# A graph attention layer on one core: fewer filler matmuls ahead of the second counts, and row steps of the sort cut in other places

## Chip, core and metric

The kernel runs on one core of a Trainium2 chip. The metric is the device time of one execution in microseconds (us), lower is better. TensorE is PE in the rows, its weight loads PEld; VectorE is DVE, ScalarE is ACT, GpSimd is POOL, SyncE is SP. A letter q behind an engine's name means its sequencer.

## What is computed

The layer has 4096 nodes with 64 features, 50,000 edges and 4 heads. Each edge carries its source's projected row to its target with the weight exp(leaky(s + d)), and the sums are divided by the sums of the weights:

```python
x_proj[h] = x @ weight[h]
src_att = np.sum(x_proj[h, src_nodes] * att_src[h], axis=-1)
dst_att = np.sum(x_proj[h, dst_nodes] * att_dst[h], axis=-1)
edge_scores[h] = src_att + dst_att
edge_scores = np.where(edge_scores > 0, edge_scores, 0.2 * edge_scores)
output[h, dst] += np.exp(edge_scores[h, i]) * x_proj[h, src]
total = np.sum(np.exp(edge_scores[h, edges_to_dst]))
output[h, dst] /= (total + 1e-8)
```

## The kernel before

Edges become one number each (a key) and are put in order twice, so that all that follows are dense matmuls. The order of instructions on each engine is the order of the source: the part is written under a manual schedule, and the semaphores between engines are set from what each instruction reads and writes.

**First sort.** 128 partitions hold up to 512 keys each. `rows` (L342) sorts each partition's keys on VectorE: fours, then merges with `merge(k)` (L242), k from 3 to 7 and at last 9, where merge k joins sorted pieces into pieces of 2^k columns. A merge step is a MIN and a MAX between two sets of columns. It is issued as three instructions: MIN over the right part of the pieces, MAX over all, MIN over the left part (`left` pieces lie in the left part). So each instruction has another one between itself and the one whose output it needs first. `runs` (L368) then merges the rows of 4 partitions: ScalarE scales two parts of the columns by a sign (L376), VectorE shuffles (L380), combines (L383), and goes through steps j = 8 to 0 (`cross`, L364, three instructions a step by `apart`, L213; or `half`, L205, a MIN and a MAX of 256 columns each), with transpositions (`turn`, L358, in two parts of 384 and 128 columns). The keys go to DRAM.

**Second sort** (`group`, L529). Four indirect DMAs fetch `raw` (L522). `wide` (L305) sorts halves of 256 columns on VectorE, its last two steps over both halves (L319), and calls `merge(9)`; `runs` merges 8 partitions. Beside it ScalarE counts keys below 32 bounds, one pass (L422) for each, into the columns of `sgn`. TensorE has nothing to do between the score matmuls (L609) and these counts. When pass 25 is done (`WARM`), `busy` (L1065) issues one small matmul that waits for it (L1069) and then `EARLY` filler matmuls of 512 columns (L1071), whose result nobody reads; then the counts matmul (`counts`, L428, L432), which needs all 32 passes, and `LATER` more fillers.

**From the counts to the blocks.** The last steps of `runs` in the second sort (L399 to L405) are `half` steps, and behind each stands one small VectorE instruction of another kind: first `st.count` (L463), which reads the counts out of PSUM, then the fields of the first block's keys (L1079, L1082, L1083), then the start of the windows (L468, L470, L471). ScalarE casts the fields to `tb` (L1084), TensorE spreads them over all partitions (L684, 12 of 16 tiles first), ScalarE copies them to `bc` (L686), VectorE compares them to one-hot matrices `oh` (L699, L701). The sorted keys go out as `ki`, and POOL fetches `win` (L522) with indirect DMAs behind their store. VectorE takes win apart (L628 to L633), the result is stored to `gat_bins` and loaded back broadcast as `bc` for the blocks 2 and on (L673).

**Blocks.** 32 blocks of 128 target nodes follow in a pipeline: one-hot matrices on VectorE, gathering matmuls (L718 to L720), exp and casts on ScalarE (L730, L732), products (L752), sums on TensorE (L816), division and store. From block 2 on each takes the same time.

Of the kernel before, what the change touches and what calls it, by code (L numbers as in the profile page):

```python
# [16 lines left out]
OP = mybir.AluOpType  # L17
# [13 lines left out]
FINE = 2  # L31
PARTS = (slice(L // 4, L), slice(0, L // 4))
WARM = 25
EARLY = 28
REST = 2
LATER = 17
KPAD = float(1 << 24)
LOW = 80
HIGH = 24
# [5 lines left out]
def av(a, off, *dims):  # L45

    return dataclasses.replace(a, offset=a.offset + off, ap=[list(a.ap[0])] + [list(d) for d in dims])
# [3 lines left out]
def kernel(ctx: ExitStack, tc: tile.TileContext, x: bass.AP, edge_index: bass.AP,  # L51
                         weight: bass.AP, att_src: bass.AP, att_dst: bass.AP, out: bass.AP):
    nc = tc.nc
    V, S, G, T = nc.vector, nc.scalar, nc.gpsimd, nc.tensor
# [46 lines left out]
    def bits(name, shift, mask):  # L101
        i = cst.tile([P, 1], I32, name=f"{name}_i")
        f = cst.tile([P, 1], F32, name=f"{name}_f")
        V.tensor_scalar(out=i[:], in0=pidx[:], scalar1=shift, scalar2=mask, op0=OP.logical_shift_right,
                        op1=OP.bitwise_and)
        G.tensor_copy(out=f[:], in_=i[:])
        return f
# [6 lines left out]
    for j in range(3):  # L114
        f = bits(f"b{j}", j, 1)
# [73 lines left out]
    class Sorter:  # L189
# [52 lines left out]
        def merge(self, k, at=0, ns=1, left=0, top=L, way=None, steps=(1, 9), meanwhile=()):  # L242


            n = 1 << k
            q, third = n // 4, n // 8
            one, two, three = way or ((self.cur + i) % 4 + 1 for i in range(3))
            segs = ((left, ns), (0, left)) if left else ((0, 1),)

            def compare(s, d, op, lower, upper, *dims, out=None):  # L250
                if out is None:
                    out = av(d, upper if op == OP.max else lower, *dims)
                V.tensor_tensor(out=out, in0=av(s, lower, *dims), in1=av(s, upper, *dims), op=op)  # L253

            for i in range(max(steps[0], 1), min(steps[1], k) + 1):
                h = n >> i
                if i == 1:
                    s, d, apart = self.a[self.cur], self.a[one], (one - two) * L
                    if k == 3:
                        for lower, op in ((q, OP.min), (q, OP.max), (0, OP.max), (0, OP.min)):  # L260
                            o = lower + (op == OP.max) * h
                            compare(s, d, op, lower, lower + h, [n, ns], [1, q],
                                    out=av(self.a[one if q <= o < 3 * q else two], o, [n, ns], [1, q]))
                    elif left:
                        low = lambda f, e: compare(s, d, OP.min, at + n * f, at + n * f + h, [n, e - f], [q, 2], [1, q],
                                                   out=av(self.a[two], at + n * f, [n, e - f], [apart + q, 2], [1, q]))
                        low(*segs[0])
                        compare(s, d, OP.max, at, at + h, [n, ns], [q, 2], [1, q],
                                out=av(d, at + h, [n, ns], [q - apart, 2], [1, q]))
                        low(*segs[1])  # L270
                    else:
                        compare(s, d, OP.min, at + q, at + 3 * q, [1, q])
                        if top < at + n:
                            compare(s, d, OP.max, at, at + h, [1, q])
                            compare(s, self.a[two], OP.max, at + q, at + 3 * q, [1, top - at - 3 * q])
                        else:
                            compare(s, d, OP.max, at, at + h, [q, 2], [1, q], out=av(d, at + h, [q - apart, 2], [1, q]))
                        compare(s, self.a[two], OP.min, at, at + h, [1, q])
                    if k > 2:
                        ends = 1 if top < at + n else 2  # L280
                        e = (at, [n, ns], [n - third, ends], [1, third])
                        S.copy(out=av(self.a[three], *e), in_=av(self.a[two], *e))
                    for f in meanwhile:
                        f()
                    self.cur = one
                    continue
                s, self.cur = self.a[self.cur], three if i % 2 else two
                d = self.a[self.cur]
                m = min((1 << (i - 1)) - 1, -(-(top - at - h) // (2 * h)))
                pairs = lambda op, f, e, a, b: compare(s, d, op, at + n * f + h * (2 * a + 1), at + n * f + h * (2 * a + 2),  # L290
                                                       [n, e - f], [2 * h, b - a], [1, h])
                if left:
                    pairs(OP.min, *segs[0], 0, m)
                    pairs(OP.max, 0, ns, 0, m)
                    pairs(OP.min, *segs[1], 0, m)
                elif i == 2:
                    pairs(OP.min, 0, 1, 0, m)
                    pairs(OP.max, 0, 1, 0, m)
                else:
                    c = 1 << (i - 3)  # L300
                    pairs(OP.min, 0, 1, 0, c)
                    pairs(OP.max, 0, 1, 0, m)
                    pairs(OP.min, 0, 1, c, m)

        def wide(self, alone, load, between, meanwhile):  # L305

            k = 8
            way = 1, 2, 3
            for at in (0, L // 2):
                self.cur = 0  # L310
                load(at)
                self.merge(k, at, way=way, steps=(1, alone))
            between()
            for i in range(alone + 1, k + 1):
                s, self.cur = self.a[self.cur], way[2] if i % 2 else way[1]
                d, h, n = self.a[self.cur], 1 << (k - i), 1 << k
                for o, op, f, e in ((0, OP.min, 0, 1), (h, OP.max, 0, 2), (0, OP.min, 1, 2)):
                    dims = [n, e - f], [2 * h, n // (2 * h) - 1], [1, h]
                    V.tensor_tensor(out=av(d, n * f + h + o, *dims), in0=av(s, n * f + h, *dims),  # L319
                                    in1=av(s, n * f + 2 * h, *dims), op=op)  # L320
            self.merge(9, meanwhile=meanwhile)

        def fours(self, n, then):
# [18 lines left out]
        def rows(self, n, then, meanwhile):  # L342

            w8, w128 = -(-n // 8) * 8, n // 128 * 128
            assert 0 < n - w128 <= 8 and w128 == 3 * 128
            ways = {3: (2, 4, 1), 4: (2, 3, 4), 5: (2, 1, 4), 6: (3, 2, 1), 7: (3, 4, 1)}
            self.fours(w8 // 4, then)
            for k in range(3, 8):
                w = w8 if k <= 3 else w128
                self.merge(k, 0, w >> k, 2 if k == 7 else 192 >> k, meanwhile=meanwhile[k],  # L350
                           way=ways[k])
                assert k not in (3, 7) or self.cur == 1
            self.apart(7, mirror=True, right=True)
            for j in range(6, -1, -1):
                self.apart(j, w128 if j > 2 else w8, 128, right=True)
            self.merge(9, top=w8, meanwhile=meanwhile[9])
# [11 lines left out]
        def runs(self, size, then, skey, to=None, fine=0, between=()):  # L368
# [4 lines left out]
            s, z = self.step()  # L373
# [4 lines left out]
            for c in PARTS:  # L378
                c = slice(L - c.stop, L - c.start)
                V.stream_shuffle(out=z[:, c], in_=s[:, c], mask=[p ^ 1 for p in range(32)])  # L380
            d = self.step()[1]
# [3 lines left out]
            s, d = self.step()  # L385
# [10 lines left out]
            todo = list(between)  # L396
            for j in range(8, fine, -1):
                if todo:
                    self.half(j)  # L399
                    todo.pop(0)(self.a[self.cur])  # L400
                else:
                    self.cross(j)
            s, d = self.step()
            d, h = to or d, 1 << fine
            for c in (L // 2, 0):  # L405
                for o, op in ((0, OP.min), (h, OP.max)):
                    V.tensor_tensor(out=av(d[:], c + o, [2 * h, L // (4 * h)], [1, h]),
                                    in0=av(s[:], c, [2 * h, L // (4 * h)], [1, h]),
                                    in1=av(s[:], c + h, [2 * h, L // (4 * h)], [1, h]), op=op)
# [119 lines left out]
    def group(pool, pp, start, between=(), busy=None, scores=None):  # L529
# [18 lines left out]
        def then():  # L548
# [4 lines left out]
            if between:  # L553
                busy(EARLY, (sel2[:], sgn[:, WARM:WARM + 1]))
            st.ps = counts(pp, sgn, 8 * NI, [sel2[:]])
            if between:
                busy(LATER)

# [89 lines left out]
    class Blocks:  # L648
# [20 lines left out]
        def load(self, b, parts=((0, NT),)):  # L669
            if b < ND:  # L670
                t = self.bcp.tile([P, 2 * NT * W2], BF16, name="bc")
                for t0, n in parts:
                    nc.sync.dma_start(out=t[:, t0 * PW:(t0 + n) * PW],  # L673
                                      in_=dataclasses.replace(bin_dram[b], offset=bin_dram[b].offset + t0 * PW,
                                                              ap=[[0, P], [1, n * PW]]))
                self.bc[b] = t
# [523 lines left out]
```

## Time and profile before

| | us |
|---|---|
| median of 3 runs | 259.88 (258.58 to 260.5) |
| the profiled execution's own time | 257.67 |
| its span, first to last instruction | 255.9 |
| granted TensorE clock, mean over the span | 0.891 of full speed |
| busy: PE 200.9, DVE 238.9, ACT 201.8, POOL 44.7 | |

Some 1.8 us of the profiled execution lie outside the span. Times in the rows are counted from the span's start. The work up to about 104 us is sorting, and the blocks fill the rest.

### The profile page before, as it was taken

To read this page: it belongs to the slowest core of one execution; us is meant where nothing else is said; L and a number is where in the kernel's file an instruction comes from. 1 tells how busy PE (TensorE), PEld (TensorE's weight loads), DVE (VectorE), ACT (ScalarE), POOL (GpSimd) and SP (SyncE) were. 2 spreads that over 40 slices of the span, in tenths; PEclk is the share of its full clock that TensorE was granted. 3 is DMA by queue.
4 is the path that set the end of the run, shared out by engine and by line. 5 is a ranking of instruction groups with operands and counts; after the bars stand their busy time and mean duration, and the time that the engine had idled before them with its cause. 6 is when DMAs were issued, how large, how long until landed. Compare 5 with 4: busy or idle time off the path is not lost.

```text
span 255.9 us, 6908 instructions
## 1 busy us (share of the span) xinstructions
PE 200.9 (79%) x2539; PEld 178.4 (70%) x2539; DVE 238.9 (93%) x682; ACT 201.8 (79%) x523; POOL 44.7 (17%) x97
## 2 busy tenths in 40 slices
PE   0004669999200599878999999999999999999995
PEld 0003339999200245667999999999999999999994
DVE  7999999928999978989999999999999999999993
ACT  2774579005889935997999999999999999999981
POOL 7788000042000000584000007500000000000000
PEclk9999985555555589999999999999999999999999
DMA  4005000010000001189768677687767768675012
GB/s 125 0 2 186 0 3 3 0 62 21 1 0 0 0 0 45 41 305 409 269 256 300 247 270 289 233 318 246 286 251 241 303 226 327 250 298 220 23 44 68
DMA packets 12422, 39.43 MB, mean 154 GB/s; under 512 B 2208, under 2 KB 7904, under 8 KB 8800
## 3 DMA queue, kind: packets, MB, share of 16 engines
q1 hardware_dynamic: 10752, 36.84, 39.4%
q10 hardware_dynamic: 928, 1.51, 1.7%
q0 software_dynamic: 704, 0.59, 1.0%
q8 instruction: 21, 0.34, 0.5%
q14 instruction: 17, 0.14, 0.2%
HBM read 33.96 MB, written 4.98 MB: 152 GB/s over the span
## 4 chain that ended last, share of the span: by engine, by line
PE 57%; DVE 27%; ACT 7%; DMA 5%; issue 2%; POOL 0%; DVEq 0%; SPq 0%; POOLq 0%; ACTq 0%
PE acc L816 20%; DVE sorted L253 11%; PE ps L719 10%; DVE sorted L240 7%; PE ps L720 6%; PE ps L718 6%; PE pt L911 5%; ACT junk L422 5%; PE warm L1071 5%; PE pt L896 3%; DMA bc<-gat_bins 2%; DVE oh L699 1%; DVE val L752 1%; DMA eS<-in_edge_index_dram 1%; ACT bc L686 1%
## 5 line engine op out<-in xcount | busy, mean ns | idle before, releaser
L732 ACT CAST xs<-ps 128x1176 bf16<-128x1176 f32 (+1 forms) x96 | 103.2, 1076 | 0.0
L752 DVE TENSOR_TENSOR val<-xs,val 128x3072 bf16<-128x3072 bf16 (+2 forms) x64 | 75.1, 1173 | 0.7
L816 PE MATMUL acc<-val,xs 128*128 128x264 bf16 x496 | 66.4, 276 | 0.7 <-DVE val L752 0.7
L718 PE MATMUL ps<-xa,oh 128*128 128x68 bf16 x512 | 51.7, 194 | 2.5 <-ACT xs L732 0.9
L816 PEld LDWEIGHTS <-xs 128*128 128x128 bf16 x496 | 46.2, 98 | 6.7 <-DVE val L752 0.8
L719 PE MATMUL ps<-adb,oh 128*128 128x132 bf16 x512 | 49.6, 220 | 0.0
L718 PEld LDWEIGHTS <-oh 128*128 128x128 bf16 x512 | 43.7, 97 | 2.9 <-DVE oh L699 1.8
L719 PEld LDWEIGHTS <-oh 128*128 128x128 bf16 x512 | 40.8, 97 | 3.0 <-issue 2.3
L699 DVE TENSOR_SCALAR oh<-bc,pF 128x3328 bf16<-128x3328 bf16 (+4 forms) x38 | 36.1, 951 | 1.9 <-ACT bc L686 1.0
L720 PE MATMUL ps<-xa,oh 128*128 128x68 bf16 x512 | 36.3, 194 | 0.4 <-DVE oh L701 0.4
L730 ACT ACTIVATE ex<-ps 128x48 bf16<-128x48 f32 (+1 forms) x192 | 33.0, 243 | 4.2 <-PE ps L719 1.5
L240 DVE TENSOR_TENSOR sorted<-sorted 128x192 f32<-128x192 f32 (+2 forms) x141 | 34.4, 326 | 0.0
L253 DVE TENSOR_TENSOR sorted<-sorted 128x128 f32<-128x128 f32 (+22 forms) x157 | 30.1, 270 | 0.4 <-ACT junk L422 0.4
L720 PEld LDWEIGHTS <-oh 128*128 128x128 bf16 x512 | 28.6, 97 | 0.9 <-DVE oh L701 0.5
L609 PEld LDWEIGHTS scores<-uv,xT 64*128 64x128 f32 x128 | 27.6, 318 | 0.4 <-issue 0.4
L609 PE MATMUL scores<-uv,xT 64*128 64x4 f32 x128 | 27.7, 353 | 0.0
L422 ACT ACTIVATE junk<-kr,nb 128x512 f32<-128x512 f32 x32 | 23.1, 722 | 0.9
L701 DVE TENSOR_SCALAR oh<-bc,pF 128x1664 bf16<-128x1664 bf16 (+4 forms) x38 | 22.4, 591 | 0.0
L432 PE MATMUL cnt_ps<-sgn,sel 128*128 128x17 f32 (+1 forms) x10 | 2.2, 346 | 22.1 <-DVE sorted L253 22.1
L911 PE MATMUL pt<-Wbd,aT 128*128 128x128 f32 x124 | 19.0, 275 | 0.0
L432 PEld LDWEIGHTS cnt_ps<-sgn,sel 128*128 128x128 f32 x10 | 2.2, 300 | 22.2 <-issue 22.0
L1069 PE MATMUL warm<-sgn,sel 128*128 128x1 f32 x2 | 0.6, 364 | 20.4 <-ACT junk L422 20.4
(161 smaller groups left out, 280.8 us busy)
## 6 DMA issues: line engine op xcount, KB each, us to landing
bc<-gat_bins SPq DMA_DIRECT2D x28, 1024.0 KB, 5.6
out_dram<-res SPq DMA_DIRECT2D x32, 128.0 KB, 2.3
xf<-in_x_dram ACTq DMA_DIRECT2D x1, 1024.0 KB, 5.8
bc<-gat_bins SPq DMA_DIRECT2D x1, 768.0 KB, 4.6
bc<-gat_bins SPq DMA_DIRECT2D x1, 640.0 KB, 5.1
bc<-gat_bins SPq DMA_DIRECT2D x1, 384.0 KB, 3.9
gat_sorted<-sorted SPq DMA_DIRECT2D x2, 128.0 KB, 1.7
gat_sorted<-ki SPq DMA_DIRECT2D x2, 128.0 KB, 1.8
```

What stands on the lines that cost most here:

```text
L240: V.tensor_tensor(out=out, in0=in0, in1=in1, op=op)
L253: V.tensor_tensor(out=out, in0=av(s, lower, *dims), in1=av(s, upper, *dims), op=op)
L422: todo = [lambda b=b: S.activation(out=junk[:], in_=v, func=ACTF.Sign, bias=nbnd[:, b:b + 1], scale=1.0, accum_out=sgn[:, b:b + 1]) for b ...
L609: T.matmul(out=scores[:, k * NB + b, :], lhsT=nodes(b), rhs=uv[:, k, :], start=(k == 0 and b == 0), stop=True, skip_group_check=True)
L699: V.tensor_scalar(out=av(oh[:], *e), in0=av(bc[:], *e), scalar1=pF[:, 0:1], scalar2=None, op0=OP.is_equal)
L718: kinds = [lambda i, t, **how: T.matmul(out=ps[:, i, P:P + XC], lhsT=hot(2 * t + 1), rhs=xa[:, t, :], **how), lambda i, t, **how: T.matmul ...
L719: lambda i, t, **how: T.matmul(out=ps[:, i, 0:S0], lhsT=hot(2 * t), rhs=adb[:, b, :], **how),
L720: lambda i, t, **how: T.matmul(out=ps[:, i, P:P + XC], lhsT=hot(2 * NT + t), rhs=xa[:, NR + t, :], **how)]
L730: S.activation(out=av(ex[:], 2 * (k * H * NT + t0), [2, n], [2 * NT, H], [1, 2]), in_=av(ps[:], P, [PW, n], [1, H], [0, 2]), func=ACTF.Exp ...
L732: S.copy(out=xs[:, t0:t0 + n, 0:P + XC], in_=ps[:, 0:n, 0:P + XC])
L752: V.tensor_tensor(out=av(val, t0 * AW, [VW, H * n], [1, Din]), in0=av(xs, S0 + t0 * XW, [XW, n], [0, H], [1, Din]), in1=av(val, t0 * AW + ...
L816: T.matmul(out=acc[:, 0:AW], lhsT=xs[:, t, 0:P], rhs=val[:, t, :], start=(t == 0), stop=(t == NT - 1), **how)
```

## The change

Two constants and four places that cut instructions differ:

```diff
-EARLY = 28
+EARLY = 14
-LATER = 17
+LATER = 18
@@ merge(): the last step of a merge of 9
                     pairs(OP.min, 0, 1, 0, c)
                     pairs(OP.max, 0, 1, 0, m)
+                    if k == 9 and i == k:
+                        pairs(OP.min, 0, 1, c, 3 * c)
+                        c *= 3
                     pairs(OP.min, 0, 1, c, m)
@@ wide(): its last step
-                for o, op, f, e in ((0, OP.min, 0, 1), (h, OP.max, 0, 2), (0, OP.min, 1, 2)):
...
+                m = n // (2 * h) - 1
+                ends = ((m // 2 + 1, m), (0, m // 2 + 1)) if i == k else ((0, m),)
+                for o, op, f, e, a, b in ((0, OP.min, 0, 1, 0, m), (h, OP.max, 0, 2, 0, m),
+                                          *((0, OP.min, 1, 2, a, b) for a, b in ends)):
...
@@ rows(): the pieces in the left part
-                self.merge(k, 0, w >> k, 2 if k == 7 else 192 >> k, meanwhile=meanwhile[k],
+                self.merge(k, 0, w >> k, (192 if k < 5 else 256) >> k, meanwhile=meanwhile[k],
@@ runs(): the first of the steps that have other work behind them
-                    self.half(j)
+                    self.cross(j) if j == 8 else self.half(j)
```

- There are 14 fillers instead of 28 between the small matmul that waits for pass 25 and the counts, and 18 instead of 17 behind the counts.
- In the merges of 5 and 6 the left part has 8 of 12 and 4 of 6 pieces instead of half of them. The merge of 7 has 2 of 3 in both kernels.
- The last MIN of the last step is cut in two in both merges of 9 and at the end of `wide`.
- The first step behind the last transposition of the second sort is `cross(8)`: MIN of columns 128 to 255 against 384 to 511, MAX of all, MIN of the rest.

The instructions of ScalarE, GpSimd and SyncE and all DMAs stand as before. What follows of the changed kernel is five lines further down in the source (L468 there is L463 here).

VectorE behind the last transposition of the second sort, before the change (`sorted` are the sort's buffers, `cnt_ps` the counts in PSUM; a bracket names the engine whose semaphore is waited for):

```order
L362 STREAM_TRANSPOSE sorted<-sorted 128x384 [waits DVE_49]
L362 STREAM_TRANSPOSE sorted<-sorted 128x128 [waits DVE_49]
L209 TENSOR_TENSOR sorted<-sorted 128x256 [waits DVE_49]
L209 TENSOR_TENSOR sorted<-sorted 128x256
L463 TENSOR_SCALAR cnt<-cnt_ps 128x33 [waits PE_49]
L209 TENSOR_TENSOR sorted<-sorted 128x2x128 [waits DVE_49]
```

The same place after the change:

```order
L367 STREAM_TRANSPOSE sorted<-sorted 128x384 [waits DVE_49]
L367 STREAM_TRANSPOSE sorted<-sorted 128x128 [waits DVE_49]
L240 TENSOR_TENSOR sorted<-sorted 128x128 [waits DVE_49]
L240 TENSOR_TENSOR sorted<-sorted 128x256 [waits DVE_49]
L240 TENSOR_TENSOR sorted<-sorted 128x128
L468 TENSOR_SCALAR cnt<-cnt_ps 128x33 [waits PE_49]
L209 TENSOR_TENSOR sorted<-sorted 128x2x128 [waits DVE_49]
```

Two instructions of 256 columns became three of 128, 256 and 128, and the first of them reads only what the first transposition wrote.

VectorE at the end of the second merge of 9, before the change:

```order
L253 TENSOR_TENSOR sorted<-sorted 128x64 [waits DVE_49]
L253 TENSOR_TENSOR sorted<-sorted 128x255 [waits DVE_49]
L253 TENSOR_TENSOR sorted<-sorted 128x191
L380 STREAM_SHUFFLE sorted<-sorted 128x384 [waits DVE_49]
L380 STREAM_SHUFFLE sorted<-sorted 128x128
L383 SCALAR_TENSOR_TENSOR sorted<-sorted,sig_104 128x384 [waits DVE_49,Activation_49]
```

The same place after the change:

```order
L253 TENSOR_TENSOR sorted<-sorted 128x64 [waits DVE_49]
L253 TENSOR_TENSOR sorted<-sorted 128x255 [waits DVE_49]
L253 TENSOR_TENSOR sorted<-sorted 128x128
L253 TENSOR_TENSOR sorted<-sorted 128x63
L385 STREAM_SHUFFLE sorted<-sorted 128x384 [waits DVE_49]
L385 STREAM_SHUFFLE sorted<-sorted 128x128 [waits DVE_49]
L388 SCALAR_TENSOR_TENSOR sorted<-sorted,sig_104 128x384 [waits DVE_49,Activation_49]
```

The MIN of 191 columns became two of 128 and 63, and the first shuffle reads nothing of the second; the SCALAR_TENSOR_TENSOR waits for ScalarE (Activation) as before.

## Rows read from the trace of the kernel before

**Rows 1.** Chain of waits, 85.9 to 113 us: start us, us, what

```profile
86.58 8.33 PE warm L1071 x28
...
99.49 2.79 ACT bc L686 x2
...
106.55 2.00 DMA gat_bins<-tb
...
108.57 3.91 DMA bc<-gat_bins
...
112.50 0.55 DVE oh L699
```

**Rows 2.** PE in order of time: start us, us, line, operation, count

```profile
86.44 4.80 PE L1071 MATMUL warm<-identb 128*128 128x512 bf16 x11
91.08 3.83 PE L1071 MATMUL warm<-identb 128*128 128x512 bf16 x17
94.75 0.30 PE L432 MATMUL cnt_ps<-sgn,sel 128*128 128x33 f32 x2
94.97 3.83 PE L1071 MATMUL warm<-identb 128*128 128x512 bf16 x17
98.63 1.47 PE L684 MATMUL ps<-tb,identb 128*128 128x256 bf16 x12
```

**Rows 3.** Stretches: length, PE, PEld, DVE, ACT, POOL busy, PEclk, DMA share, GB/s

```profile
91.00:92.00 1.00, 1.00 (x6) 0.45 (x5) 1.00 (x5) 0.84 (x3) 0.00 (x0) 0.97 0.00 0
112.00:114.00 2.00, 1.10 (x22) 0.94 (x20) 1.40 (x4) 2.00 (x8) 1.83 (x6) 1.00 1.03 433
```

**Rows 4.** ACT in order of time: last counting pass, cast of the fields

```profile
91.68 0.18 ACT L422 ACTIVATION_READ_ACCUMULATOR junk<-kr,nb 128x1 f32 x1
97.12 0.41 ACT L1084 CAST tb<-t 128x256 bf16<-128x256 int32 x1 [5.25 <-DVE t L1083]
```

**Rows 5.** DVE in order of time, 82 to 106 us, in brackets idle time and releaser

```profile
82.10 0.77 DVE L362 STREAM_TRANSPOSE sorted<-sorted 128x384 f32<-128x384 f32 x2
82.79 0.79 DVE L240 TENSOR_TENSOR sorted<-sorted 128x128 f32<-128x128 f32 x3
...
92.27 0.77 DVE L362 STREAM_TRANSPOSE sorted<-sorted 128x384 f32<-128x384 f32 x2
93.08 0.76 DVE L209 TENSOR_TENSOR sorted<-sorted 128x256 f32<-128x256 f32 x2
95.09 0.19 DVE L463 TENSOR_SCALAR cnt<-cnt_ps 128x33 f32<-128x33 f32 x1 [1.25 <-PE cnt_ps L432]
...
99.40 0.89 DVE L407 TENSOR_TENSOR ki<-sorted 128x128 int32<-128x128 f32 x4
...
102.30 0.62 DVE L699 TENSOR_SCALAR oh<-bc,pF 128x1536 bf16<-128x1536 bf16 x1 [0.39 <-ACT bc L686]
...
105.84 0.22 DVE L628 TENSOR_SCALAR t<-win 128x128 int32<-128x128 int32 x1
```

**Rows 6.** The first fetch of win on POOL, and the four fetches' landing times

```profile
102.88 0.95 POOL L522 DMA_INDIRECT win<-gat_sorted,to  x1 [43.72 <-DMA gat_sorted<-ki]
DMA to landing us min/median/max: 2.5/3.0/6.3
```

**Rows 7.** Ends of wide and of the second merge of 9: DVE and ACT in order of time

```profile
64.46 0.62 DVE L319 TENSOR_TENSOR sorted<-sorted 128x254 f32<-128x254 f32 x2
65.11 0.63 DVE L253 TENSOR_TENSOR sorted<-sorted 128x128 f32<-128x128 f32 x2
71.30 0.91 ACT L376 ACTIVATE sorted<-sorted,sig 128x384 f32<-128x384 f32 x2 [0.92 <-DVE sorted L253]
72.00 0.88 DVE L383 SCALAR_TENSOR_TENSOR sorted<-sorted,sig 128x384 f32<-128x384 f32 x2
```

**Rows 8.** Stretches of the merges of 6 and of 7, VectorE alone

```profile
15.55:18.86 3.31, 3.31 (x20) 1.00 0.02 0
18.86:22.76 3.90, 3.90 (x22) 1.00 0.75 264
```

More of the change, by code (lines that the diff above doesn't have):

```diff
@@ L316, in wide @@
                 d, h, n = self.a[self.cur], 1 << (k - i), 1 << k
-                for o, op, f, e in ((0, OP.min, 0, 1), (h, OP.max, 0, 2), (0, OP.min, 1, 2)):
-                    dims = [n, e - f], [2 * h, n // (2 * h) - 1], [1, h]
-                    V.tensor_tensor(out=av(d, n * f + h + o, *dims), in0=av(s, n * f + h, *dims),
-                                    in1=av(s, n * f + 2 * h, *dims), op=op)
+                m = n // (2 * h) - 1
+                ends = ((m // 2 + 1, m), (0, m // 2 + 1)) if i == k else ((0, m),)
+                for o, op, f, e, a, b in ((0, OP.min, 0, 1, 0, m), (h, OP.max, 0, 2, 0, m),
+                                          *((0, OP.min, 1, 2, a, b) for a, b in ends)):
+                    at, dims = n * f + h * (2 * a + 1), ([n, e - f], [2 * h, b - a], [1, h])
+                    V.tensor_tensor(out=av(d, at + o, *dims), in0=av(s, at, *dims), in1=av(s, at + h, *dims), op=op)
             self.merge(9, meanwhile=meanwhile)
```

## Prediction

> **What bounds the kernel now.** I read the chain of waits first. From 86 us it runs through the fillers: 28 of them for 8.33 us, and then, over the spread fields, ScalarE's `bc`, the store to gat_bins and the load back, to the one-hot of block 2 at 112.50 [rows 1]. From there on block follows block, so what shifts that one-hot shifts the end. In time order, PE begins its fillers at 86.44; ten steps to the start of the eleventh and one more bring it to 91.08, 0.42 us each; the 17 from there to the counts at 94.75 take 0.216 each [rows 2]. The granted clock rose between them: 0.97 over 91 to 92 us [rows 3]. So the fillers serve to raise the clock from 1.2 to 2.4 GHz, and 17 of the 28 ran after it had risen. What the counts need was long there: ScalarE's last pass ended at 91.68 + 0.18 = 91.86 [rows 4], 2.9 us before the counts began. VectorE, which reads them, was ready about 93.8 and idled 1.25 us until 95.09 [rows 5]. Behind the counts PE ran 17 fillers to 98.63 [rows 2], though the fields it spreads next were cast at 97.12 + 0.41 = 97.53 [rows 4]: a second wait, of 1.1 us.
>
> **Fillers, 28 to 14.** The first eleven run to 91.08, three more at 0.216 to 91.73. The counts then wait for ScalarE (91.86) and start at about 91.90, 2.85 earlier; with their 0.30 the result is there by 92.2. VectorE is then late next, not PE.
>
> **The step behind the last turn.** `half(8)` starts 93.08 - 92.27 = 0.81 after its transpositions start. A `cross` behind a turn already stands in this trace: it starts 82.79 - 82.10 = 0.69 after them, because its first MIN overlaps the second transposition (it starts 0.08 before that ends, `half` 0.04 after) [rows 5]. Its three instructions last 0.79; an instruction that waits for nothing starts about 0.09 before the end, so 0.70 to the next. With nothing else changed VectorE reads the counts at 92.27 + 0.69 + 0.70 = 93.66 instead of 95.09. An instruction more on 512 columns costs 0.03 to 0.10: two last 0.76, three 0.79, four 0.89 [rows 5], mean 0.065; in this step it is inside the 0.79.
>
> **The other cuts of the sort** move everything before that by a little.
> - End of `wide`: the merge started 65.11, 0.03 after the MIN ended at 65.08 [rows 7], so it lost about 0.12 against an overlap of 0.09. With a second half in between the loss goes and 0.065 comes: -0.05.
> - End of the merges of 9: the shuffles can start earlier, but the combine at 72.00 waits also for ScalarE's first part, which starts 71.30, when the last MIN is done [rows 7]. A cut MIN ends 0.065 later, so ScalarE and the combine do: +0.07 in each sort, +0.14 if nothing gives. The bounds are -0.06 each (if the combine were held by the shuffles alone) and +0.10.
> - Two to one in the merges of 5 and 6: the merge of 6 takes 3.31 for 6 steps, 0.552 a step, the merge of 7, which has this cut already, 3.90 for 7, 0.557 [rows 8]. Eleven steps at a difference of 0.005 are 0.06; I take nothing, bounds -0.1 and +0.1.
>
> Sum -0.05 + 0.14 = +0.09, bounds -0.3 and +0.3. The counts are read at 93.75: -1.34 us. They are ready at 92.2 or, ScalarE's passes shifting by the same 0.09, 92.3, so 1.4 us cover this.
>
> The Trainium skill, VectorE: DVE Perf Modes, section The DRAIN you can't avoid, speaks against these cuts: the flush behind each VectorE instruction comes with or without a semaphore, so one should count instructions and not waits. By it the cuts in `wide` and behind the turn would gain none of their 0.12, the counts would be read 0.24 later, and the sum below would be -1.5. Rows 5 and 7 disagree: the distance behind an instruction was 0.04 or -0.08 by whether the next needed its output.
>
> **From the counts to block 2.** Two branches shift differently.
> - Spread. The cast ends at 97.53 - 1.34 = 96.19. Fillers: the first follows the counts' start by 0.22, 92.2, and 18 at 0.215 (17 took 98.63 - 94.97 = 3.66) end at 96.07. The spread starts at about 96.23 instead of 98.63: -2.40. The eighteenth filler costs nothing since the cast is later still; without that cover it costs 0.22. ScalarE's copies and the second one-hot (102.30) follow, and VectorE would reach L628 at 105.84 - 2.40 = 103.44.
> - Windows. L628 needs `win`, fetched from the sorted keys behind `ki` (99.40). That is VectorE's branch and gains only 1.34. The fetch was issued at 102.88 and lands 2.5 later at the least [rows 6]: 105.38, so it had up to 0.46 to spare before L628 at 105.84. Now it lands at 104.04, and L628 waits for it until 104.08: -1.76. If it had landed just in time, L628 gains 1.34 only. I take 2.5, since this is the first of four fetches and the later ones find the queue used.
>
> The store (2.00) and the load (3.91) [rows 1] start on L628 and move with it; before the load's end VectorE idled, so nothing else is late there. Sum: 1.8 us less. Against the profiled execution that is 257.67 - 1.8 = 255.9. The median is 2.2 us above that execution; the stage is the same, so I take the 1.8 off the median: 258.1, 0.7% less. A measurement of this kernel can tell about 1%, or 2.6 us, from no change.
>
> **Rivals.**
> - *The window binds fully.* If `win` landed only at 105.84, or the keys' store and fetch take longer in their new place, the gain is 1.34 or less: 258.5 to 259. For it: no row gives this fetch's own landing. Against: the least of four is 2.5.
> - *The clock rises at another moment.* A rise 0.42 later turns a filler of 0.216 into one of 0.42, so it delays the counts of before by 0.21, while the changed kernel hides it until 14 fillers at 0.42 (86.44 + 5.91 = 92.35) and the counts are done at 92.7, still ahead of 93.75. A rise 1.6 later makes the gain 1.8 + 0.8 = 2.6, 257.3; 1.6 earlier makes it 1.0, 258.9. For it: the runs of before differ by 1.9 us. One trace shows only one moment.
> - *Too few fillers, slower.* If the clock rises only after more work than 14 fillers and the counts, or is taken back because of the gap before the counts, the 18 later fillers take 18 x 0.42 = 7.6 and the spread starts at 99.8 instead of 98.63, +1.2; the spread and the first gathers, 1.5 us of PE work [rows 2] and as much again, at half the clock add 1.5 to 3: 262.6 to 264. It decides from a rise later than about 95. Against: the clock rose while the eleventh filler ended, and it held through 112 to 114 us with PE busy only 1.10 of 2.00 [rows 3]; the gap before the counts is under 0.2 us.
> - *The cuts of the sort cost more than they gain* (0.3): 258.4, inside the range.
>
> The Trainium skill, TensorE: Matmul & The Clock Gate, Part 1, says that the point at which the clock is released varies between runs of one kernel, as the monitor does not start with the kernel. By it the second rival is real in both directions; no trace here shows a second moment.
>
> **How the numbers follow.** Forecast (gain of 1.4 to 2.4): 0.58. Window binds or other small gain (0.3 to 1.4): 0.16. Late rise, gain above 2.4: 0.17. No gain within 0.3, as with an early rise and a full window: 0.04. Too few fillers: 0.05. Faster by over 1% needs 2.6 us: the late rise and the noise of the two medians at the edge of the forecast, 0.22. Slower: 0.05. Same: 0.73. The range 256.8 to 259.4 takes in gains from 0.5 to 3.1.
>
> **What would show it.** In the changed profile: 14 fillers from about 86.5, the last ones at 0.216; counts within 0.2 us of ScalarE's last pass; VectorE without idle time before it reads them, about 93.7; the spread directly behind the cast at about 96.2; and VectorE idle about 0.6 before L628 (now five lines further down), waiting for `win`. The gain at the counts should be 1.3 and at the first one-hot of block 2 1.8. Wrong would be: fillers of 0.42 behind the counts, an idle VectorE before the counts, or a one-hot of block 2 that moved by under 1 us.

## The result, and the profile after

The changed kernel takes 255.66 us (255.41 to 258.57, 19 runs) where the kernel before, timed beside it, takes 259.19 (258.44 to 260.5, 19 runs): a ratio of 0.9867, 95% interval [0.9847, 0.9887], or 3.5 us less. The forecast was 1.8 us less, 258.1, with a range from 256.8 to 259.4. The two profiled executions, 257.67 before and 255.53 after, differ by 2.14 only. So there are two questions: did the stage move as worked out, and where does the rest of the 3.5 us come from?

The chain of waits after, over the stretch of [rows 1] (columns as there):

```profile
86.79 4.71 PE warm L1076 x14
...
92.56 3.89 PE warm L1076 x18
...
97.19 2.79 ACT bc L691 x2
...
101.65 2.43 DMA win<-gat_sorted,to
...
105.07 1.53 DMA gat_bins<-tb
...
106.62 3.72 DMA bc<-gat_bins
...
110.37 0.59 DVE oh L704
```

A fetch of `win` stands in the chain now, which it did not before, and the one-hot of block 2 comes at 110.37 instead of 112.50: 2.13 earlier, as much as the two executions differ by. TensorE (PE) in order of time answers to [rows 2]:

```profile
86.65 4.85 PE L1076 MATMUL warm<-identb 128*128 128x512 bf16 x14
92.18 0.38 PE L437 MATMUL cnt_ps<-sgn,sel 128*128 128x33 f32 x2 [0.68 <-issue]
92.39 4.05 PE L1076 MATMUL warm<-identb 128*128 128x512 bf16 x18
96.34 1.47 PE L689 MATMUL ps<-tb,identb 128*128 128x256 bf16 x12
```

The counts start 2.57 us earlier than in [rows 2] and the spread 2.29. The clock, by stretches as in [rows 3]:

```profile
89.00:90.00 1.00, 1.00 (x3) 0.30 (x2) 1.00 (x4) 0.97 (x3) 0.00 (x0) 0.50 0.00 0
90.00:91.00 1.00, 1.00 (x6) 0.51 (x5) 1.00 (x6) 0.97 (x3) 0.00 (x0) 0.98 0.00 0
```

It rose from 1.2 to 2.4 GHz about 90.0, some 1 us earlier than in [rows 3]. ScalarE's last pass and cast, as in [rows 4]:

```profile
91.89 0.19 ACT L427 ACTIVATION_READ_ACCUMULATOR junk<-kr,nb 128x1 f32 x1
...
95.89 0.41 ACT L1089 CAST tb<-t 128x256 bf16<-128x256 int32 x1 [3.81 <-DVE t L1088]
```

The cast ends at 96.30 and the spread follows at 96.34: the second wait of [rows 2] is gone too. VectorE (DVE), as in [rows 5] and [rows 7]:

```profile
65.27 6.21 DVE L253 TENSOR_TENSOR sorted<-sorted 128x128 f32<-128x128 f32 x27
...
72.16 0.88 DVE L388 SCALAR_TENSOR_TENSOR sorted<-sorted,sig 128x384 f32<-128x384 f32 x2
...
92.45 0.76 DVE L367 STREAM_TRANSPOSE sorted<-sorted 128x384 f32<-128x384 f32 x2
93.14 0.78 DVE L240 TENSOR_TENSOR sorted<-sorted 128x128 f32<-128x128 f32 x3
93.84 0.18 DVE L468 TENSOR_SCALAR cnt<-cnt_ps 128x33 f32<-128x33 f32 x1
...
104.17 0.36 DVE L633 TENSOR_SCALAR t<-win 128x128 int32<-128x128 int32 x1 [0.50 <-DMA win<-gat_sorted,to]
```

No idle time stands in front of the counts' read (1.25 us in [rows 5]), and 0.50 us in front of L633, waiting for `win`. Both were forecast.

### The profile page after: what moved, and what is told of

Same layout as the page of the kernel before. It is cut to its first block, busy times and chain, and to the rows that moved or that the text cites. A ratio compares the mean times of both kernels' runs of the same rounds, so it can differ in the third digit from the quotient of the medians.

```text
span 253.7 us, 6886 instructions
## 1 busy us (share of the span) xinstructions
PE 198.3 (78%) x2526; PEld 177.2 (70%) x2526; DVE 239.1 (94%) x686; ACT 201.6 (79%) x523; POOL 44.0 (17%) x97
## 4 chain that ended last, share of the span: by engine, by line
PE 56%; DVE 27%; ACT 7%; DMA 4%; issue 4%; DVEq 0%; SPq 0%; ACTq 0%
PE acc L821 21%; DVE sorted L253 12%; PE ps L724 11%; DVE sorted L240 7%; PE ps L725 6%; PE ps L723 6%; PE pt L916 5%; ACT junk L427 5%; PE warm L1076 3%; PE pt L901 3%; DMA bc<-gat_bins 1%; DVE oh L704 1%; DMA eS<-in_edge_index_dram 1%; ACT bc L691 1%; DVE val L757 1%
## 5 line engine op out<-in xcount | busy, mean ns | idle before, releaser
L240 DVE TENSOR_TENSOR sorted<-sorted 128x192 f32<-128x192 f32 (+2 forms) x144 | 35.2, 319 | 0.0
L253 DVE TENSOR_TENSOR sorted<-sorted 128x128 f32<-128x128 f32 (+23 forms) x159 | 30.2, 266 | 0.4 <-ACT junk L427 0.4
L916 PEld LDWEIGHTS pt<-Wbd,aT 128*128 128x128 f32 x124 | 16.3, 191 | 0.0
```

What stands on the lines that cost most here:

```text
L240: V.tensor_tensor(out=out, in0=in0, in1=in1, op=op)
L916: T.matmul(out=self.pt[:, k * P:(k + 1) * P], lhsT=self.aT[b][:, k * P:(k + 1) * P], rhs=Wbd[:, k, :], start=True, stop=True, skip_group_c ...
```

## Experiments

They ran on six chips, each beside the kernel before. The chips are numbered here in the order of the runs, and nothing but these runs tells them apart:

| chip | runs | kernel before, us | changed kernel, us |
|---|---|---|---|
| 1 | e1 to e4 | 257.95 (23 runs) | 255.62 |
| 2 | e5 to e8 | 259.02 (26) | 255.76 |
| 3 | f1 to f4 | 259.20 (25) | 255.84 |
| 4 | g1 to g3 | 259.47 (17) | |
| 5 | h1, h2 | 257.08 (6) | |
| 6 | i1 | 257.28 (9) | |

The changed kernel takes nearly the same on all; the kernel before is 1 to 2.4 us slower on chips 2 to 4 than on the others.

### The halves of the change (e1 to e4)

e1 is the kernel before, unchanged, and e4 the changed one.

> The kernel before, unchanged, timed again with a new profile. Theory A (the moment of the clock's rise differs between executions, and the first profile of before had an early one): a ratio of 1.00, times spread over about 2 us (258.4 to 260.5), and a profile in which VectorE's wait for the counts is as much longer or shorter than 1.25 us as its own time lies above or below 257.67. Theory B (the first profile was low for another reason, such as the input loads or a DMA): the wait for the counts is again 1.2 to 1.3 us whatever the time is.

> The changed kernel unchanged, on the same chip. Every theory: ratio 0.986 to 0.988, times of 255.4 to 256.2 apart from single ones above 257. Theory A: its profile has VectorE going into the counts without idle time, wherever the clock rises.

e2 is the kernel before with `EARLY = 14` and `LATER = 18` alone; e3 has the new cuts of the sort with the old constants (its line numbers are those of after).

> Only the numbers of fillers are changed (14 and 18), the sort is as before. Theory A: nearly the whole gain, ratio 0.987 to 0.989 (256.0 to 256.5), with times that spread over less than 1 us apart from single ones. Rival C (the cuts of the sort carry more than was forecast): 0.991 to 0.995.

> Only the cuts of the sort, with 28 and 17 fillers as before. Theory A: the counts come when the fillers let them, so nothing is gained, ratio 0.998 to 1.002, and the times spread over 2 us as before's do. Rival C: 0.992 to 0.996.

Measured: e1 257.89, ratio 1.0003 [0.9982, 1.0024]; e2 255.76, 0.9932 [0.9908, 0.9956]; e3 257.19, 0.999 [0.9971, 1.001]; e4 255.62, 0.9918 [0.9894, 0.9942]. The fillers alone make the gain; the cuts make nothing that can be told. The ratios of e2 and e4 miss what was expected of them, and e2's lies in rival C's range, because the kernel before takes 257.95 here and not 259.19; that the cuts carry nothing is told by e3, and by e2 and e4 taking the same time within 0.14 us. TensorE of e1, and of e4:

```profile
86.70 8.73 PE L1071 MATMUL warm<-identb 128*128 128x512 bf16 x28
95.27 0.30 PE L432 MATMUL cnt_ps<-sgn,sel 128*128 128x33 f32 x2
```

```profile
86.71 5.78 PE L1076 MATMUL warm<-identb 128*128 128x512 bf16 x14
92.33 0.30 PE L437 MATMUL cnt_ps<-sgn,sel 128*128 128x33 f32 x2
```

Here the clock rose later than in the first two traces, so 14 fillers took 5.78 us instead of 4.85. The counts' read stood at 93.91 in e4 against 93.84, since VectorE is late last; with 28 fillers in front of the counts each of nine traces has its own moment: the fillers took 7.57 to 9.05 us, and the counts' read came at 94.30 to 95.61, behind 0.34 to 1.81 us of idle time on VectorE (1.50 in e1). Of theory A in e1 this half came true; the other did not: e1's wait is 0.25 us longer than in the first profile of before, its time 0.70 longer.

### Must the fillers stand right in front of the counts? (e5 to e8)

e5 is the kernel before with all 28 fillers let go earlier, behind pass 17; e6 is the changed kernel with 4 in front; e7 and e8 are both kernels unchanged.

```diff
-WARM = 25
+WARM = 17
```

```diff
-EARLY = 14
+EARLY = 4
```

> The kernel before with one constant changed: the 28 fillers start behind counting pass 17 instead of pass 25, 6.8 us earlier, so the clock can rise and all 28 can end before ScalarE's last pass. Theory A (the counts of before wait for fillers whose end moves with the moment of the rise): nearly the whole gain comes without taking one filler away, 255.8 to 256.4, and the times lie within about 0.6 us. Rival E (fewer fillers gain by themselves, through power or through PE's use of memory): no gain, 257.5 to 258.5.

> The changed kernel with 4 instead of 14 fillers ahead of the counts, so that PE stands idle for about 3.5 us before them. Too few fillers, as priced in the prediction: the clock is not up, the 18 fillers behind the counts take 0.42 each at first, the spread comes 0.5 to 3.5 us later than in the changed kernel, 256.5 to 259. Rival (the clock rises at its moment whatever PE does): 255.5 to 255.8 as with 14.

> The kernel before, unchanged, a third time. The first comparison had 259.19, the second 257.95. Theory A: the median is again between 257.0 and 259.5 and follows the moment of the rise, 0.5 us later for each us that the rise comes later; the first 12 steps on VectorE and the transfers are as in the other profiles.

> The changed kernel unchanged, again. Theory A: 255.5 to 255.8 in every job, whatever before's median is, because VectorE and no longer the fillers sets the moment of the counts; the ratio moves between 0.986 and 0.993 with before's median.

Measured: e5 257.89, 0.9946 [0.9926, 0.9966], where 255.8 to 256.4 had been expected; e6 258.25, 0.9963 [0.9942, 0.9985]; e7 258.92, 0.9987 [0.9968, 1.0007]; e8 255.76, 0.9854 [0.9824, 0.9883]. TensorE of e5 in order of time, then its stretches:

```profile
79.56 7.71 PE L1071 MATMUL warm<-identb 128*128 128x512 bf16 x28
91.86 0.61 PE L432 MATMUL cnt_ps<-sgn,sel 128*128 128x33 f32 x2 [4.59 <-issue]
92.28 5.81 PE L1071 MATMUL warm<-identb 128*128 128x512 bf16 x17
97.93 1.25 PE L684 MATMUL ps<-tb,identb 128*128 128x256 bf16 x10
```

```profile
83.00:86.00 3.00, 3.00 (x15) 1.37 (x14) 3.00 (x13) 2.87 (x9) 0.00 (x0) 1.00 0.00 0
86.00:89.00 3.00, 1.27 (x6) 0.39 (x4) 3.00 (x13) 2.90 (x7) 0.00 (x0) 1.00 0.00 0
89.00:92.00 3.00, 0.14 (x1) 0.17 (x2) 3.00 (x12) 2.67 (x8) 0.00 (x0) 0.58 0.00 0
92.00:95.00 3.00, 3.00 (x9) 1.29 (x10) 2.97 (x12) 0.00 (x0) 0.00 (x0) 0.50 0.03 5
```

The fillers raised the clock and then TensorE stood idle for 4.59 us until ScalarE's last pass; the clock fell back to 1.2 GHz in that gap. The counts are as early as in the changed kernel, but the 17 fillers behind them start at 1.2 GHz, take 5.81 us instead of the 3.83 of [rows 2], and the spread starts at 97.93. e5's 257.89 is also what rival E named for no gain; but the kernel before takes 259.02 here, and VectorE reads the counts at 93.66 without idle time behind all 28 fillers, so the early counts do not need fewer of them. e6 comes out alike from the other side: with 4 fillers its clock had not risen by the counts, the 18 later ones took 5.55 us, and the spread started at 97.93 too. So the gain needs both: few enough fillers not to stand in the way, and enough, right in front of the counts, to have the clock up. Not all that e5 and e6 lose is lost there: both also have the late releases of the next section.

### What slows the kernel before on some chips (e3 against e7, f1 to f4)

e3 (chip 1) and e7 (chip 2) stand alike up to the spread (98.36 and 98.21) and even to the store (106.28 and 106.13). Yet e3's profiled execution took 257.22 us and e7's 258.85. ScalarE (ACT) in e3 and then the clock and busy times of two stretches there:

```profile
104.18 0.35 ACT L735 ACTIVATE ex<-ps 128x48 bf16<-128x48 f32 x2
```

```profile
103.90:107.30 3.40, 2.52 (x26) 1.78 (x25) 3.12 (x11) 3.00 (x8) 2.26 (x2) 1.00 0.19 46
107.30:110.70 3.40, 3.02 (x36) 2.54 (x36) 3.15 (x11) 3.39 (x4) 1.24 (x2) 1.00 0.43 121
```

The same in e7, with TensorE's matmuls that ScalarE waits for ahead of them:

```profile
103.34 0.35 PE L720 MATMUL ps<-xa,oh 128*128 128x68 bf16 x6
```

```profile
105.99 0.31 ACT L730 ACTIVATE ex<-ps 128x48 bf16<-128x48 f32 x2 [1.83 <-PE ps L720]
```

```profile
103.90:107.30 3.40, 1.43 (x20) 1.09 (x18) 2.27 (x9) 1.57 (x6) 2.11 (x2) 1.00 0.23 53
107.30:110.70 3.40, 3.22 (x17) 2.14 (x15) 2.07 (x4) 2.57 (x7) 0.00 (x0) 0.51 0.40 123
```

The second gather of block 0 ends at 103.34 + 0.35 = 103.69 by its rows, but ScalarE, which waits for nothing else by the trace, starts at 105.99: its release came 2.3 us late. That leaves TensorE a hole (busy 1.43 of 3.40 us against 2.52), and behind the hole the clock falls a second time, to 0.51 over 107.3 to 110.7, while TensorE spreads the fields of block 1. Late release and fall together are the 1.6 us by which e7 ended later than e3. The fall does not always follow: e6 has the late release (2.4 us) and as deep a hole, and keeps 2.4 GHz:

```profile
104.80:108.20 3.40, 1.40 (x14) 0.92 (x11) 2.29 (x8) 2.35 (x7) 0.36 (x1) 1.00 0.17 45
108.20:111.60 3.40, 3.11 (x32) 2.50 (x32) 2.56 (x9) 3.21 (x4) 0.70 (x1) 1.00 0.76 260
```

e5 shows the same (1.36 of 3.40 us, then 1.00).

Late releases of 2.3 to 2.4 us stand in all traces of a kernel on chips 2 to 4 whose spread starts at 97.8 or later (e5, e6 and e7 on chip 2; g1, below, has 3.0), and in none on chip 1. In e8 only the third gather's release is late, by 0.7 us, for ScalarE 0.19 us of idle time. Of the two first profiles, the trace of before that the prediction was read from has no late release (ScalarE's second exp, without idle time), and that of the changed kernel has the third gather's, like e8:

```profile
104.45 0.35 ACT L730 ACTIVATE ex<-ps 128x48 bf16<-128x48 f32 x2
```

```profile
103.79 0.29 ACT L735 ACTIVATE ex<-ps 128x32 bf16<-128x32 f32 x2 [0.25 <-PE ps L725]
```

Next came what they hang on: f1 puts the spread of the changed kernel at the old place, f2 takes the fillers between the second and third gather out of the kernel before, f3 gives it five more in front of the counts, f4 is the changed kernel.

```diff
-LATER = 18
+LATER = 27
```

```diff
-            if c == 1:
-                busy(2)
```

```diff
-EARLY = 28
+EARLY = 33
```

> The changed kernel with 27 fillers behind the counts instead of 18: the counts stay early (about 92.1 us), but the spread starts at 92.1 + 27 x 0.213 = about 97.9 us, where it stood in the three traces in which TensorE's releases of the second and third gather came 1 to 2.4 us late. Theory P (such a late release comes with the place of the spread, on the chips that show it): late releases again, and about 258.0 us, as with few fillers in front. Theory C (it comes from how short ago the clock was low): TensorE is at 2.4 GHz from about 90 us on here, so no late release, and 255.7 + 1.6 = 257.0 to 257.4 us. On a chip where the kernel before shows none, both give 257.0 to 257.4.

> The kernel before without the two fillers behind the second gather. Theory B (these fillers, which use a buffer of the block sums, are what holds TensorE's releases up): no late release, and 1.2 us less than the kernel before on a chip that shows late releases. Theory P: the releases of the gathers stay late and the time stays within 0.4 us of the kernel before; the third gather starts at the one-hot's end either way.

> The kernel before with 33 fillers in front of the counts instead of 28. All five added ones run at 0.213 us, so counts, spread and the end move 1.07 us later: 1.0 to 1.1 us above the kernel before if every us of the spread is a us of the end, which the forecast took for granted. If the late releases hang on the place of the spread (theory P) and this place is free of them, 0 to 0.3 us above the kernel before on a chip that shows them. A rise of the clock at another moment changes a single trace by up to 0.9 us.

> The changed kernel once more, beside the others on this chip: 255.5 to 255.9 us, spread at 96.2 to 96.5 us, no late release.

Measured: f1 258.12, 0.9965 [0.995, 0.9981]; f2 259.51, 1.0003 [0.9982, 1.0023]; f3 259.08, 1.0014 [0.999, 1.0038]; f4 255.84, 0.9882 [0.9858, 0.9905]. TensorE and ScalarE of f1:

```profile
92.16 5.99 PE L1076 MATMUL warm<-identb 128*128 128x512 bf16 x27
97.99 1.47 PE L689 MATMUL ps<-tb,identb 128*128 128x256 bf16 x12
```

```profile
105.77 0.31 ACT L735 ACTIVATE ex<-ps 128x48 bf16<-128x48 f32 x2 [1.67 <-PE ps L725]
```

The clock is up early and the counts are early, but the spread is at 97.99 and the second exp waits 1.67 us as in e7: theory P holds, theory C falls. With theory C goes the thought that the clock's history is to blame. f2 has the wait (1.96 us) without the fillers, so theory B falls. f3 has it in its trace (1.92), but its runs fall in two groups, six at 258.81 to 259.19 and four at 260.56 to 261.18; the four, of which its trace is one, show mean clocks of 0.888 and 0.993, the others 0.906 to 0.907 and 0.999 to 1.0. The profiles of e7 and f3, which have the second fall, show 0.887 and 0.993. Read so, late releases and second fall together cost about 1.7 us there, and f3's median hardly moved, where 1.0 had been expected, because most of its runs escaped a fall that by its clocks nearly every run of the kernel before has on this chip. That reading rests on the mean clocks alone. The late release by itself costs time too: the eight runs of before on chips 2 and 3 whose clocks (0.89 to 0.9, and 1.0) show no fall take 258.27 to 258.91, where the median on chip 1 is 257.95. f4 came as expected but for a late release of its third gather (0.8 us).

### What ends the late release (g1 to g3, h1, h2, i1)

g1 (before) and g3 (after) put three VectorE instructions ahead of block 0's first product, g2 four fillers behind the third gather of the kernel before.

```diff
+        for i in range(3):
+            V.tensor_scalar(out=t0[:], in0=t0[:], scalar1=1, scalar2=None, op0=OP.bitwise_and)
         blocks.product(0, 0)
```

```diff
-            if c == 1:
-                busy(2)
+            if c:
+                busy(2 * c)
```

> The kernel before with three VectorE instructions on a scratch tile (512 columns each, by the 0.22 us of 128 columns some 0.5 us each, so about 1.5 us) ahead of block 0's first product; nothing that TensorE's gathers wait for moves. Theory W (the finished gathers are held until the first sum matmul, which waits for this product, comes to TensorE): on a chip that shows late releases the second gather's comes 1.5 us later too, some 3.8 us behind its modelled end. Theory D (TensorE stops for a length of its own): still 2.3 to 2.4 us behind it. The time is 1.2 to 1.6 us above the kernel before by both, since unpacking win is queued behind the product on VectorE.

> The kernel before with four more fillers behind the third gather, so that TensorE has work up to the first sum matmul (4 x 0.213 = 0.85 us; the hole was about 0.7 us). Theory W in its form 'a finished matmul is released when more work follows': no late release, and on a chip that shows them 1.0 to 1.3 us less than the kernel before. Theory D: the second gather's release 2.3 to 2.4 us late as before, time within 0.4 us of the kernel before.

> The changed kernel with the same three VectorE instructions ahead of block 0's first product. In its traces on chips with late releases only the third gather's came late, by 0.7 to 0.8 us, when the first sum matmul started. Theory W: that grows by about 1.0 to 1.5 us with the product. Theory D: it stays at 0.8 us or less. The time is 0.4 to 1.5 us above the changed kernel: unpacking win waits 0.5 us for win anyhow.

Measured: g1 259.61, 1.0024 [0.9996, 1.0053]; g2 260.19, 1.0019 [0.9987, 1.0052]; g3 256.44, 0.988 [0.9841, 0.9919]. ScalarE of g1, and of g2:

```profile
106.35 0.32 ACT L730 ACTIVATE ex<-ps 128x48 bf16<-128x48 f32 x2 [2.55 <-remote]
```

```profile
106.47 0.32 ACT L730 ACTIVATE ex<-ps 128x48 bf16<-128x48 f32 x2 [1.82 <-PE ps L720]
```

In g1 the gather's rows end at 103.33, so the release was 3.0 us late. The three instructions have 256 columns, not 512, and moved the product by 1.1 us, not 1.5; by theory W the release would then be some 3.4 us late (2.3 + 1.1, an estimate), by theory D 2.3. In g2 it was 2.3 us late, but the four fillers were no work behind the gather. They wait for TensorE's own release of it, as the profile has it:

```profile
106.53 1.02 PE L1071 MATMUL warm<-identb 128*128 128x512 bf16 x4 [1.19 <-PE ps L720]
```

They started 0.06 us behind ScalarE's exp, so g2 does not test theory W; it shows that the late releases hold TensorE up as well. In g3 the third gather's stayed 0.7 us late. Theory D fits g2 and g3 but not g1, theory W neither g1 nor g3. The times were missed too: g1 is 0.1 us above the kernel before, where both theories had 1.2 to 1.6, and g2 is 0.7 above, where they had 0.4 at the most; only g3 lies where it was expected.

h1 and i1 (before) and h2 (after) keep GpSimd's fetches of `win` out of the stretch with nine instructions ahead of them.

```diff
+        for i in range(9):
+            G.tensor_scalar(out=kb0[:], in0=kb0[:], scalar1=1, scalar2=None, op0=OP.add)
         win = Windows(cst, stretches.to[0][:], 1)
```

> The kernel before with nine GpSimd instructions of 128 columns on a scratch tile (about 1.04 us each, behind the last fields at about 97 us) ahead of the fetches of win, so that these start at about 106 us instead of 102.4. Theory F (TensorE's releases are held up while GpSimd works through these fetches): on a chip that shows late releases those of block 0's gathers come on time, and ScalarE's second exp at about 104.2 us has no idle time before it. Theory N (nothing to do with the fetches): the second gather's release is 2.3 us late as before. By both, unpacking win waits for the fetch, so L628 and the end come about 3 us later than in the kernel before.

> The changed kernel with the same nine GpSimd instructions. Theory F: the third gather's release, 0.7 to 0.8 us late in the changed kernel on chips that show late releases, comes on time. Theory N: still 0.7 to 0.8 us late. The time is some 3 to 4.5 us above the changed kernel's 255.7 by both.

> The kernel before with the nine GpSimd instructions ahead of the fetches of win once more. Only on a chip whose runs of the kernel before show the second fall of the clock does it tell anything new: there theory F has the second gather's release on time (within 0.1 us of its modelled end), theory N has it 2.3 us late. On another chip no late release, and 2.7 us above the kernel before, as in the first such run.

Measured: h1 259.82, 1.0099 [1.0073, 1.0124]; h2 258.27, 1.006 [1.0031, 1.0088]; i1 259.16, 1.007 [1.0038, 1.0102]. h1 is 2.7 us above the kernel before, i1 1.9, and h2 2.6 above the changed kernel's 255.7, a little less than the 3, 2.7 and 3 to 4.5 expected. Chips 5 and 6 show no late release in any trace, so the question of the fetches stays open. But h1 shows the second half of the mechanism by itself. Its stretches:

```profile
105.00:108.70 3.70, 1.46 (x19) 0.99 (x18) 2.11 (x8) 2.05 (x6) 2.94 (x3) 1.00 0.14 35
108.70:112.10 3.40, 3.40 (x16) 2.30 (x17) 2.62 (x6) 2.21 (x3) 0.00 (x0) 0.51 0.30 91
```

Here the late `win` makes the hole (TensorE busy 1.46 of 3.70 us), with every release on time, and the clock falls behind it all the same. So a hole brings the fall on a chip without late releases too. That it need not is shown by e5 and e6; what decides is open.

## Why the prediction was wrong

The stage came out nearly as worked out (2.13 us instead of 1.8); what failed is the last step, from the stage to the median.

- **The counts.** Forecast: read at 93.75 without idle time, VectorE late last. Measured 93.84, none. In e2, e4 and e8, whose clocks rose at other moments, 93.75 to 93.91.
- **The cuts of the sort.** Forecast +0.09, no part of the gain; e3 says 0.999 [0.9971, 1.001]. The step behind the turn starts 93.14 - 92.45 = 0.69 behind the transpositions, as forecast, and lasts the 0.70 forecast. The Trainium skill, VectorE: DVE Perf Modes, section The DRAIN you can't avoid, says that the flush behind an instruction can't be skipped by leaving out semaphores. By that the step would have gained nothing, and these rows disagree, as [rows 5] did. The same section adds that a next instruction that is not held starts earlier, and with that they agree. The merge of 9 in the second sort cost nothing instead of 0.07: from its start to the combine 72.16 - 65.27 = 6.89, as in [rows 7]. The one in the first sort cost it: from the shuffle to the combine 0.78 us in e3 (33.36 to 34.14) against 0.70 before (33.25 to 33.95).
- **Spread and `win`.** Forecast: spread at 96.23, L633 at 104.08 waiting for a fetch of 2.5. Measured 96.34, 104.17, fetch 2.43, idle 0.50.
- **Store and load.** "The store (2.00) and the load (3.91) start on L628 and move with it" was mis-sized: the store now takes 1.55 from issue to the load's issue (105.07 to 106.62), the load 3.72. Against that, unpacking `win` took 0.90 instead of 0.71 (104.17 to 105.07; 105.84 to 106.55 in [rows 1, 5]). With L633 1.67 earlier than L628 was, that makes 1.67 + 0.47 + 0.18 - 0.19 = 2.13 at the one-hot of block 2. VectorE, which idled 0.71 us in front of that one-hot before, has no idle time there now, so a still earlier load would gain little. Why the store is quicker can be read in all 20 traces: before, its packets (107.74 to 108.20) lie beside those of the third fetch of `win` (107.43 to 108.01); after, they go ahead of them (105.89 to 106.25, the fetch 106.45 to 107.00). The store took 1.54 to 1.55 in the nine traces where the two don't meet and 1.73 to 2.06 in the eleven where they do, whichever kernel it was: g1, a kernel before with the store out of the way, 1.54; g3, a changed one with both together, 2.03.
- **"The stage is the same, so I take the 1.8 off the median."** This is the step that failed. The profiled execution of before was 1.5 us faster than the median of its 19 runs, and faster than each of them. The forecast saw the gap (2.2 us then), gave no reason for it and carried it over to the changed kernel: 255.9 for the execution became 258.1 for the median. The changed kernel has no such gap, its median lies 0.13 us above its profiled execution. The runs show a reason: late releases behind block 0's gathers and the second fall of the clock, 1.6 us in e7 against e3 and 1.7 between the two groups of f3, of which that trace has neither. The changed kernel puts the spread 2.3 us earlier and loses at most 0.25 us of ScalarE's time to a late release. So the gain is 2.2 to 2.3 us where the kernel before has none (e2 and e4 on chip 1), and 3.3 to 3.5 where it has (e8, f4 and the first comparison). That the 19 runs of before had them is argued from their times, 258.44 and up, which are those of chips 2 to 4; their clocks were not listed. The likely reason why the profile differs is the chip, which the record does not name: 257.67 lies below every run of before on chips 2 to 4 (258.26 and up) and among those of chips 1, 5 and 6 (256.60 to 259.33), while the changed kernel's own profile has the late third release that only traces from chips 2 to 4 show. What makes the releases late is open. Two of the changed kernel's 19 runs, 257.37 and 258.57, show mean clocks of 0.993 and 0.986, so it doesn't escape every time.
- **The rivals.** The clock does rise at other moments, as the Trainium skill (TensorE: Matmul & The Clock Gate, Part 1) has it: 28 fillers in front of the counts took 7.57 to 9.05 us. That gave up to 1.5 us between nine traces (idle time of VectorE 0.34 to 1.81). But the profile of before, with 1.25, lies in the middle of them, so the moment of the rise is not why it was faster than all its runs. A gain above 2.4 us, which this rival had named, came for another reason. *Too few fillers* is a real edge, shown by e6: with 4 the spread starts at 97.93. It was priced too high: 258.25 instead of 262.6 to 264, as its fillers ran at 0.21 us each from 95.6 us on, and of that 258.25 a part is the late release.

## What to carry to other kernels

A profile whose own time lies below every timed run leaves something out; look for it, or forecast for both cases, before a gain read from it is taken off the median. Fillers that raise the clock have to reach up to the work they are for: 14 did, 28 that ended 4.6 us early did not, and those that outlast the last counting pass delay the counts. When a stage moves, look at which DMAs it now meets or leaves in a queue: that was 0.47 us here, a fifth of the gain in the trace.

## What the runs showed of the hardware

- On three chips of six TensorE's releases behind a gather came 2.3 to 2.4 us late (3.0 in g1) by the ends of its matmuls' rows; on the others the same program shows none. What waits for them is late on ScalarE (1.83 us idle in e7) and on TensorE itself (1.19 in g2). It hangs on where the gathers stand (spread at 97.8 or later against 96.2 to 96.3), not on the clock's rise (f1) or the fillers between the gathers (f2). Whether work behind the gathers would end it was not tested, as g2's fillers were held too. Whether it has to do with GpSimd's fetches was tried and not settled: h1 and i1 ran on chips without it. What causes it is open.
- A hole in TensorE's work between gathers and sums can be followed by a second stretch at 1.2 GHz: busy 1.43 of 3.40 us in e7 and 1.46 of 3.70 in h1, then 0.51 of full speed over 3.4 us. Busy 2.52 of 3.40 us in the same place (e3) kept 2.4 GHz, but so did 1.36 (e5) and 1.40 (e6).
- The mean clock of a run is read with care: e8's is 0.998 although its first fillers took 0.43 us each as at 1.2 GHz; the record of the low stretch is missing there.
